# Eight of eleven chunks as seven products in three feed-forward layers, with a ring home for the half-width units and the norm's buffer as an eleventh slot

## The chip, the cores and the metric

The kernel runs on one core of a Trainium2 chip. The metric is the device time of one execution in microseconds (us); three runs of the kernel before gave 1053.86, 1053.05 and 1052.99, with a median of 1053.05. The engines are PE (matrix products; PEld is the loading of its stationary operand), DVE and ACT (elementwise work), POOL (a little elementwise work) and SP (issues the DMAs).

## The reference

Two layers over a residual stream x of 256 rows by 1024. Layer 0 mixes with forgetting attention (FoX), layer 1 with latent attention (MLA), whose shared key and value side is computed once from the x that leaves layer 0.

```python
def swiglu(x, w_in, w_out):                 # D_FF = 2816
    h = x @ w_in
    gate, up = h[..., :D_FF], h[..., D_FF:]
    return (silu(gate) * up) @ w_out

for i in range(2):
    if i == 1: k_nope, k_rope, v = shared_kv(x, ...)      # kv_down and kv_up
    x = LN(ALPHA * x + 0.5 * swiglu(x, ffn1_w_in[i], ffn1_w_out[i]))
    x = LN(ALPHA * x + (fox if i == 0 else mla)(x, ...))
    x = LN(ALPHA * x + 0.5 * swiglu(x, ffn2_w_in[i], ffn2_w_out[i]))
    gate = sigmoid(x @ ple_w_gate[i] + ple_b_gate[i])
    x = LN(ALPHA * x + gate * (p[i] @ ple_w_proj[i]))     # "PLE"
```

## The kernel before

**Every product is three.** An operand in fp32 is split into a high part, written by ACT in the type fp32r (line 242), and a low part, which DVE gets by subtracting the high one (line 243). `mm3` then issues high by high, high by low and low by high (line 590 is each single matmul). x itself is transposed on PE and split in the same way into `xT` (lines 603 and 607).

**Weights are a stream.** They arrive in raw tiles of 1 MB (three buffers, issued on SP's queue) and are split in units of 1024 columns into ten slots, `hl0` to `hl9`. Some buffers that a stage does not need (`ota`, `otb`, `qk`, `fs`) are lent to the stream as further slots and reclaimed later. A raw buffer is free again when its last unit is split. The class `Stream` plans the order: it keeps a clock for each engine, and whenever PE has been given another three matmuls (`pump`, line 358) it emits the next split if the unit's raw tile should have arrived, a slot is free, and DVE and ACT are at most 1.6 us behind PE on its clocks. If PE needs a unit that is not split yet, the split is emitted at once (`use`, line 370). So the order of instructions on ACT and DVE is fixed when the program is built, by these clocks. The two attention stages have a written order (`FOX`, `ORDER`), in which splits stand as steps of their own.

**A feed-forward layer** (`ffn`, line 698) runs over 11 chunks of 256 hidden columns. Chunks 0 and 1 are made first by `H`: x is the stationary operand and the weights move, for the upper 128 rows (t = 0) and, after x's lower rows are transposed, for t = 1. Each of these chunks has four units, written here (chunk, unit): (0,0) to (0,3) and (1,0) to (1,3). Chunks 2 to 10 are made by `HT` in three groups, (2,3,4), (5,6,7), (8,9,10): 96 matmuls of 128x256 each.

**The way back to 1024 columns** exists in two forms. `W` (line 906) takes a chunk's activations as stationary operand and multiplies with two units of `w_out`: eight products of 128x512, so 24 matmuls. `sums` (line 835) does the same with seven products of sums, so 21 matmuls. For it DVE first adds the activations (`add`, lines 820 to 825, in a tile `P`), splits 896 columns of them into a "home" (one of `ota`, `otb`, `qk`, `fs`), and adds the weights in the raw tile and a tile `ts` (lines 274, 280, 282); a chunk's weights are then four units, three of 1024 columns and one of 512 (key `ws`). The sums run in two batches, behind the first and the second group of `HT`; `combine` then adds the seven results into x. The chunks that use `W` are the last three, 8 to 10, and those in `early`: 0, 1 and 2 in the first layer (`cold`), 0 and 1 in layer 1's first feed-forward (`kv`, where the key and value work runs too), and 1 in the two second feed-forwards. `W` runs at the end for t = 0, then the norm of x's upper rows (`ln`, `ln_apply`, line 682), then `W` for t = 1 and the norm of the lower rows. The norm's gain and bias lie in a tile `gb`, loaded at chunk 4 (`load_gb`).

**Behind layer 0's second feed-forward** stand the PLE (line 1025) with eight units `pg` 0 to 7, and the `kv` layer's start. `post` (line 1049) multiplies the sigmoid, which ACT makes, with the projected embedding and takes the norm's statistics; `ln_apply` follows. In this stretch the units of `kv_down` (`kd` 0 to 3, 640 columns) and the first units of `H` are split too, between the norms.

## Time and profile before

| what | value |
| --- | --- |
| median of three runs | 1053.05 us (1052.99 to 1053.86) |
| the profiled execution: time, span | 1056.31 us, 1054.5 us |
| granted PE clock in it | 0.999 |
| busy in the span: PE, DVE, ACT, POOL | 1043.3, 872.7, 584.5, 57.5 us |
| read from HBM | 200.55 MB, 191 GB/s over the span |

The span is the part of the execution that the profile covers; 1.8 us of the execution lie around it. A row of a group of instructions gives the line, the engine, the operation, output and inputs by the program's names, the shape, the count, then busy us and mean ns of one, then the idle time of the engine ahead of them and what ended it. A row of a timeline gives start and length in us and, in square brackets, the idle time just before. A matmul's length in these rows holds its fill and drain; neighbours overlap, so their pace is read from the starts.

### The profile page before, as it was taken

The page shows a single profiled execution, that of the slowest core. Times are in us where ns is not written, and L with a number is a line of the kernel's source. Part 1 is how long each engine was busy: PE and PEld are TensorE (multiplying, and loading weights), DVE is VectorE, ACT ScalarE, POOL GpSimd, SP SyncE. Part 2 cuts the span into 40 slices and gives each one's busy share as a digit, 9 for nine tenths or more (in the row PEclk, how much of TensorE's full clock was granted, in tenths as well). Part 3 has the DMA queues.
Part 4 walks back from the last instruction along what each step waited for, and adds up shares of the span by engine and source line. Part 5 has one row for each costly group of instructions (what it writes and reads, how often), then busy time and mean ns, then how long its engine had stood idle before and what let it go on. Part 6 is the DMA issues. An engine that isn't in the chain of part 4 may idle for free.

```text
span 1054.5 us, 17598 instructions
## 1 busy us (share of the span) xinstructions
PE 1043.3 (99%) x7097; PEld 955.8 (91%) x7097; DVE 872.7 (83%) x1280; ACT 584.5 (55%) x889; POOL 57.5 (5%) x88
## 2 busy tenths in 40 slices
PE   9999999999999999999999999999999999999996
PEld 8999898999889999998899999988999889899986
DVE  5797976868898989968978898778887989899776
ACT  5555554556745555663564655536776564656621
POOL 0000000122400000000130000000000000000000
PEclk9999999999999999999999999999999999999999
DMA  7765486444637373764574637633444565555622
GB/s 279 284 228 208 160 277 246 155 146 151 221 132 275 139 259 134 256 232 159 179 274 158 240 125 248 235 109 105 151 155 165 188 213 194 199 197 213 208 113 80
DMA packets 37477, 202.75 MB, mean 192 GB/s; under 512 B 3970, under 2 KB 9874, under 8 KB 16532
## 3 DMA queue, kind: packets, MB, share of 16 engines
q1 hardware_dynamic: 37396, 201.63, 53.9%
q8 instruction: 56, 0.92, 0.3%
q14 instruction: 25, 0.20, 0.1%
HBM read 200.55 MB, written 1.06 MB: 191 GB/s over the span
## 4 chain that ended last, share of the span: by engine, by line
PE 71%; DVE 2%; ACT 1%; issue 0%; DVEq 0%; ACTq 0%
PE h L590 37%; PE y L590 23%; PE tr L590 8%; PE tr L594 2%; PE h L594 0%; DVE hl L243 0%; DVE x L682 0%; DVE tr L1688 0%; ACT qk L603 0%; ACT P L1313 0%; DVE h L1295 0%; DVE y L1295 0%; DVE hl L254 0%; ACT xT L1606 0%; DVE PT L607 0%
## 5 line engine op out<-in xcount | busy, mean ns | idle before, releaser
L590 PE MATMUL h<-xT,hl 128*128 128x256 f32 x3384 | 397.0, 279 | 0.2 <-DVE hl L303 0.2
L590 PEld LDWEIGHTS h<-xT,hl 128*128 128x128 f32 x3384 | 393.4, 189 | 1.9 <-ACT xT L603 0.6
L243 DVE TENSOR_TENSOR hl<-raw,hl 128x1024 fp32r<-128x1024 f32 (+3 forms) x289 | 336.3, 1195 | 52.5 <-ACT hl L242 51.1
L242 ACT ACTIVATE hl<-raw 128x1024 fp32r<-128x1024 f32 (+3 forms) x289 | 286.3, 1030 | 75.6 <-PE y L590 31.8
L590 PE MATMUL y<-hl,g 128*128 128x512 f32 x432 | 100.3, 390 | 0.0
L590 PEld LDWEIGHTS y<-hl,g 128*128 128x128 f32 x432 | 80.6, 188 | 16.3
L590 PE MATMUL y<-hl,otb 128*128 128x512 f32 x264 | 70.2, 398 | 0.0
L590 PE MATMUL h<-hl,xT 128*128 128x512 f32 (+2 forms) x300 | 65.2, 370 | 0.0
L590 PEld LDWEIGHTS h<-hl,xT 128*128 128x128 f32 x300 | 52.5, 188 | 9.3
L590 PEld LDWEIGHTS y<-hl,otb 128*128 128x128 f32 x264 | 48.2, 188 | 10.3 <-DVE otb L607 0.3
L254 DVE TENSOR_TENSOR hl<-raw,hl 128x1024 fp32r<-128x1024 f32 (+2 forms) x42 | 50.2, 1199 | 1.5 <-ACT hl L250 1.4
L590 PE MATMUL y<-hl,ota 128*128 128x512 f32 x192 | 49.9, 394 | 0.0
L674 POOL TENSOR_TENSOR rs<-ve,mhalf 128x1 f32<-128x1 f32 x16 | 15.1, 944 | 621.3 <-DVE ve L673 621.3
L590 PE MATMUL y<-hl,xT 128*128 128x512 f32 (+3 forms) x258 | 47.8, 333 | 0.0
L250 ACT ACTIVATE hl<-raw 128x1024 fp32r<-128x1024 f32 (+2 forms) x42 | 43.1, 1029 | 6.8 <-DVE raw L282 5.6
L603 ACT ACTIVATE xT<-tr 128x512 fp32r<-128x512 f32 x28 | 16.2, 597 | 53.2 <-PE tr L594 53.1
L590 PE MATMUL tr<-xT,hl 128*128 128x256 f32 x384 | 45.6, 278 | 0.0
L590 PEld LDWEIGHTS tr<-xT,hl 128*128 128x128 f32 x384 | 44.9, 188 | 0.3
L243 DVE TENSOR_TENSOR hl<-ts,hl 128x1024 fp32r<-128x1024 f32 (+1 forms) x47 | 43.4, 958 | 2.0 <-ACT hl L242 2.0
L799 ACT ACTIVATE P<-h 128x512 f32<-128x512 f32 x33 | 19.7, 598 | 45.1 <-PE h L590 45.0
L590 PEld LDWEIGHTS y<-hl,xT 128*128 128x128 f32 x258 | 39.8, 188 | 4.5 <-ACT xT L603 0.4
L590 PEld LDWEIGHTS y<-hl,ota 128*128 128x128 f32 x192 | 35.0, 188 | 6.6
(284 smaller groups left out, 1442.3 us busy)
## 6 DMA issues: line engine op xcount, KB each, us to landing
raw<-in_ffn_in_dram SPq DMA_DIRECT2D x85, 1024.0 KB, 4.9
raw<-in_ffn_out_dram SPq DMA_DIRECT2D x44, 1024.0 KB, 4.9
raw<-in_pg_dram SPq DMA_DIRECT2D x8, 1024.0 KB, 5.9
raw<-in_mo_dram SPq DMA_DIRECT2D x8, 1024.0 KB, 4.8
raw<-in_kq_dram SPq DMA_DIRECT2D x8, 640.0 KB, 3.9
gb<-in_ln_g_dram SPq DMA_DIRECT2D x8, 512.0 KB, 5.7
gb<-in_ln_b_dram SPq DMA_DIRECT2D x8, 512.0 KB, 6.5
raw<-in_fk_dram SPq DMA_DIRECT2D x4, 1024.0 KB, 5.4
```

The costliest lines, as they stand in the source:

```text
L242: nc.scalar.activation(hi, src, AF.Copy)
L243: nc.vector.tensor_tensor(lo, src, hi.bitcast(F32), op=ALU.subtract)
L250: nc.scalar.activation(hi, src, AF.Copy)
L254: nc.vector.tensor_tensor(lo, src, hi.bitcast(F32), op=ALU.subtract)
L590: self.nc.tensor.matmul(out, lhsT, rhs, start=start, stop=stop)
L594: self.nc.tensor.transpose(out, in_, self.ident)
L603: self.nc.scalar.activation(hi, src, AF.Copy)
L674: nc.gpsimd.tensor_tensor(rs, ve, self.mhalf, op=ALU.pow)
L799: nc.scalar.activation(gt, ps, AF.Silu)
```

## The change

- In the three feed-forward layers that are not `cold`, `early` is empty: chunks 0 to 7 all go by seven products. That converts chunk 1 in both second feed-forwards and chunks 0 and 1 in the `kv` layer, four chunks in all. The batches become (0,2,3,4) and (1,5,6,7).
- The homes are taken in the order `fs`, `qk`, `ota`, `otb`, in the `kv` layer too four of them; the last two are reclaimed only behind `H`.
- The unit of 512 columns (`ws` unit 3) no longer takes a slot but a tile of the `g4` ring (6 buffers of 4 KB).
- `gb` is lent to the stream from chunk 2 to chunk 8, as an eleventh slot, and the norm's gain and bias are loaded at chunk 10. This holds for the cold layer as well.
- In `add`, between ACT's high part and DVE's low part, a weight sum may be emitted (`between_sums`), where before only a waiting low part could.
- With other tags used first, the tiles move in memory: `ota` from byte 161248 to 178272 of a partition, `otb` from 178016 to 186720, `qk` from 186464 to 169696, `gb` from 169760 to 155104, `ts` from 155104 to 163552; `fs` stays.

```diff
@@ -43,7 +43,7 @@
 )
 ENDS = ((0, 512), (512, 768), (768, 1024))
 GROUPS = ((2, 3, 4), (5, 6, 7), (8, 9, 10))
-HOMES = ("ota", "otb", "qk", "fs")
+HOMES = ("fs", "qk", "ota", "otb")
 WS_ORDER = (1, 0, 2, 3)
 VRING = ((0, 0), (1, 1), (1, 2), (2, 2))
 FOX = (
@@ -138,7 +138,7 @@
     def pump(self, *a, **k):
         pass
 
-    lend = reclaim = check = load = busy = pair = follow = split = split_pieces = ahead = later = split_now = fill = pump
+    between_sums = lend = reclaim = check = load = busy = pair = follow = split = split_pieces = ahead = later = split_now = fill = pump
     between, hl, hold = {}, {}, False
 
 
@@ -179,6 +179,7 @@
         self.at = 0
         self.stop = None
         self.fixed = 80
+        self.side = False
 
     def load(self, n=NRAW):
         while self.loaded < len(self.groups) and self.loaded < self.done + n:
@@ -192,14 +193,14 @@
 
     def ahead(self):
 
-        if self.ready == len(self.order) or not self.slots or self.rest is not None:
+        if self.ready == len(self.order) or not self.free() or self.rest is not None:
             return
         if self.arrives.get(group_of(self.order[self.ready]), 1e12) <= self.pe_t + 500:
             self.split(half=True)
 
     def fill(self, n):
 
-        while self.ready < min(self.at + n, len(self.order)) and self.slots and group_of(self.order[self.ready]) in self.raw:
+        while self.ready < min(self.at + n, len(self.order)) and self.free() and group_of(self.order[self.ready]) in self.raw:
             self.split()
 
     def split_now(self):
@@ -224,9 +225,12 @@
         while self.sums_left(key):
             self.add(g)
         src, parts, n = unit_of(key, self.raw[g], self.sums.get(g))
-        slot = self.slots.pop(0)
-        self.slot_of[key] = slot
-        w = self.place(key, slot)
+        if self.aside(key):
+            w = self.pool.tile([128, 2, 512], F32R, tag="g4", name="g4", bufs=6)
+        else:
+            slot = self.slots.pop(0)
+            self.slot_of[key] = slot
+            w = self.place(key, slot)
         hi, lo = w[:parts, 0, :n], w[:parts, 1, :n]
         shape = src.shape
         if len(shape) == 3:
@@ -261,6 +265,22 @@
             both()
         self.pair(n)
         self.split_done(key, w)
+
+    def aside(self, key):
+        return self.side and key[0] == "ws" and key[-1] == 3
+
+    def free(self):
+        return self.slots or self.aside(self.order[self.ready])
+
+    def between_sums(self):
+
+        if self.rest is not None:
+            self.later()
+        elif self.ready < len(self.order) and not self.hold:
+            key = self.order[self.ready]
+            g = group_of(key)
+            if self.sums_left(key) and self.arrives.get(g, 1e12) <= self.pe_t + 500:
+                self.add(g)
 
     def sums_left(self, key):
         return key[0] == "ws" and self.added.get(group_of(key), 0) < 3
@@ -328,8 +348,8 @@
 
     def retire(self):
         if self.pending is not None and self.left[self.pending] == 0:
-            t = self.slot_of.pop(self.pending)
-            if t not in self.kept:
+            t = self.slot_of.pop(self.pending, None)
+            if t is not None and t not in self.kept:
                 self.slots.append(t)
         self.pending = None
 
@@ -357,7 +377,7 @@
 
     def pump(self):
 
-        if self.ready == len(self.order) or not self.slots or self.hold or self.order[self.ready] == self.stop:
+        if self.ready == len(self.order) or not self.free() or self.hold or self.order[self.ready] == self.stop:
             return
         arrival = self.arrives.get(group_of(self.order[self.ready]), 1e12)
         if arrival <= self.pe_t + 500 and max(self.act_t, self.dve_t) <= self.pe_t + SLACK_NS:
@@ -373,7 +393,7 @@
         i = self.index[key]
         self.at = max(self.at, i + 1)
         while self.ready <= i:
-            assert self.slots, (key, self.slot_of)
+            assert self.free(), (key, self.slot_of)
             self.split()
             self.pe_t = max(self.pe_t, self.dve_t)
         self.pump()
@@ -701,10 +721,11 @@
         nc, S = self.nc, self.S
         at = at or {}
         g, gT, forms = {}, {}, {}
-        homes = HOMES[:3] if kv else HOMES
-        S.reclaim(*homes)
-        S.fixed = 150
-        early = (0, 1, 2) if cold else (0, 1) if kv else (1,)
+        homes = HOMES
+        S.reclaim(*(homes if cold else homes[:2]))
+        S.fixed, S.side = 150, not cold
+        early = (0, 1, 2) if cold else ()
+        plain = early + tuple(range(NCH - STAG, NCH))
         summed = [c for c in range(NCH - STAG) if c not in early]
 
         def H(c, t, at=None, what=None, sweeps=0):
@@ -826,7 +847,7 @@
             S.busy(dve=700)
             tag, o = self.home(homes)
             self.high(o[:, 0, :], f[:, 128:1024])
-            S.later()
+            S.between_sums()
             self.low(o[:, 0, :], o[:, 1, :], f[:, 128:1024])
             forms[c] = tag, o
 
@@ -914,7 +935,7 @@
                             z[t][n],
                             lambda i: gT[c][:, i, 256 * kt + 128 * t : 256 * kt + 128 * t + 128],
                             lambda i: w[:, i, 512 * n : 512 * n + 512],
-                            (t, c, kt) == (0, early[0], 0), (c, kt) == (NCH - 1, 1),
+                            (t, c, kt) == (0, plain[0], 0), (c, kt) == (NCH - 1, 1),
                         )
 
         both = (0, 1)
@@ -935,6 +956,7 @@
                 self.kv_down(1)
             H(0, 1, sweeps=SW_H01)
             H(1, 1)
+            S.reclaim(*homes[2:])
         n = NCH
 
         turns = (
@@ -947,7 +969,12 @@
             for c in group:
                 for f in at.get(c, ()):
                     f()
-                if c == 4:
+                if c == 2:
+                    S.lend("gb")
+                if c == 8:
+                    S.reclaim("gb")
+                if c == 10:
+                    S.check("gb")
                     self.load_gb(li, lni)
                 if c == 10 and kv:
                     self.kv_transpose_rope()
@@ -960,7 +987,7 @@
             if i < 2:
                 if i == 1 and kv:
                     self.flush()
-                sums([c for c in summed if (c < 5) == (i == 0)], ("h", x))
+                sums([c for c in summed if (c < 5 and (cold or c != 1)) == (i == 0)], ("h", x))
                 x = 1 - x
             if i == 1:
                 S.lend(*after)
```

In the changed file the lines move: a matmul is line 610, a split's low part 247, the norm's four steps 702, the PLE's product with the sigmoid 1076.

Three places show how the order moves. The first is PE in layer 0's second feed-forward: chunk 1 on its way back to 1024 columns. Before, at the start of the last stage, it is 24 matmuls with the chunk's activations in `g4` and two units of `w_out`:

```order
L590 MATMUL y3_5059<-hl9_4891,g4_4131 128x512 x3
L590 MATMUL y0_5060<-hl9_4891,g4_4131 128x512 x3
L590 MATMUL y1_3984<-hl9_4891,g4_4131 128x512 x3
L590 MATMUL y2_3985<-hl9_4891,g4_4131 128x512 x3
L590 MATMUL y3_5059<-hl0_4903,g4_4131 128x512 x3
L590 MATMUL y0_5060<-hl0_4903,g4_4131 128x512 x3
L590 MATMUL y1_3984<-hl0_4903,g4_4131 128x512 x3
L590 MATMUL y2_3985<-hl0_4903,g4_4131 128x512 x3
```

After, in the second batch of sums, with the activations' sums in `fs`, three units in slots and the fourth in the ring:

```order
L610 MATMUL y1_3992<-hl3_4336,fs_4141 128x512 x3
L610 MATMUL y2_3993<-hl3_4336,fs_4141 128x512 x3
L610 MATMUL h1_4528<-hl8_4348,fs_4141 128x512 x3
L610 MATMUL y3_3990<-hl8_4348,fs_4141 128x512 x3
L610 MATMUL tr0_3994<-hl5_4363,fs_4141 128x512 x3
L610 MATMUL y0_3991<-hl5_4363,fs_4141 128x512 x3
L610 MATMUL tr1_3995<-g4_4375,fs_4141 128x512 x3
```

Eight lines of three matmuls have become seven.

The second place is DVE in the last stage of the same layer, at the end of the norm of x's upper rows (x0) and the transposed copy of them. Before, `pg` 0 to 5 have been split ahead of this norm, and `pg` 6 and 7 (`hl1` and `hl4` here) stand behind it:

```order
L682 SCALAR_TENSOR_TENSOR x0_69<-x0_69,mv_5150,gb_3854 128x512
L682 SCALAR_TENSOR_TENSOR x0_69<-x0_69,rs_5152,gb_3854 128x512
L243 TENSOR_TENSOR hl1_5184<-raw_5082,hl1_5184 128x1024
L243 TENSOR_TENSOR hl4_5193<-raw_5082,hl4_5193 128x1024
L607 TENSOR_TENSOR xT_75<-tr0_5198,xT_75 128x512
L607 TENSOR_TENSOR xT_75<-tr1_5208,xT_75 128x512
L663 SCALAR_TENSOR_TENSOR x1_70<-x1_70,y1_3984 128x512
```

After, only `pg` 0 to 4 are split ahead of the norm; `pg` 5 (`hl8` here) stands between the two copies, and `pg` 6 and 7 behind the norm of x's lower rows (x1), where before `kd` 0 to 3 were:

```order
L702 SCALAR_TENSOR_TENSOR x0_69<-x0_69,mv_5157,gb_4925 128x512
L702 SCALAR_TENSOR_TENSOR x0_69<-x0_69,rs_5159,gb_4925 128x512
L627 TENSOR_TENSOR xT_75<-tr0_5197,xT_75 128x512
L247 TENSOR_TENSOR hl8_5207<-raw_5081,hl8_5207 128x1024
L627 TENSOR_TENSOR xT_75<-tr1_5212,xT_75 128x512
L683 SCALAR_TENSOR_TENSOR x1_70<-x1_70,y1_3992 128x512
L684 BN_STATS st_5222<-x1_70 128x6
```

The third place is DVE in layer 0's PLE and at the `kv` layer's `H`. Before, behind the norm of x0, it splits (0,0) to (0,2) (`hl7`, `otb`, `qk`), copies xT, splits (0,3) (`fs`) and (1,0) (`hl2`), and then starts on the PLE's product for x1, which the norm of x1 follows:

```order
L243 TENSOR_TENSOR hl7_5371<-raw_5196,hl7_5371 128x1024
L243 TENSOR_TENSOR otb_5380<-raw_5196,otb_5380 128x1024
L243 TENSOR_TENSOR qk_5391<-raw_5281,qk_5391 128x1024
L607 TENSOR_TENSOR xT_75<-tr0_5394,xT_75 128x512
L607 TENSOR_TENSOR xT_75<-tr1_5401,xT_75 128x512
L243 TENSOR_TENSOR fs_5414<-raw_5281,fs_5414 128x1024
L243 TENSOR_TENSOR hl2_5425<-raw_5295,hl2_5425 128x1024
L1049 TENSOR_TENSOR g4_5429<-g4_5429,ota_5012 128x512
L663 SCALAR_TENSOR_TENSOR x1_70<-x1_70,g4_5429 128x512
```

After, `kd` 3 (`hl1`) comes behind the norm of x0, then (0,0) to (0,2) (`hl9`, `hl4`, `hl3`) around the copy, and then at once the product for x1:

```order
L247 TENSOR_TENSOR hl1_5387<-raw_5210,hl1_5387 128x640
L247 TENSOR_TENSOR hl9_5395<-raw_5291,hl9_5395 128x1024
L627 TENSOR_TENSOR xT_75<-tr0_5398,xT_75 128x512
L627 TENSOR_TENSOR xT_75<-tr1_5405,xT_75 128x512
L247 TENSOR_TENSOR hl4_5418<-raw_5291,hl4_5418 128x1024
L247 TENSOR_TENSOR hl3_5429<-raw_5322,hl3_5429 128x1024
L1076 TENSOR_TENSOR g4_5433<-g4_5433,ota_5056 128x512
```

and (0,3) (`otb`) and (1,0) (`hl8`) come behind that product's norm:

```order
L702 SCALAR_TENSOR_TENSOR x1_70<-x1_70,rs_5444,gb_5237 128x512
L702 SCALAR_TENSOR_TENSOR x1_70<-x1_70,mv_5442,gb_5237 128x512
L702 SCALAR_TENSOR_TENSOR x1_70<-x1_70,rs_5444,gb_5237 128x512
L1443 TENSOR_SCALAR ve_5480<-ss_5479 128x1
L247 TENSOR_TENSOR otb_5510<-raw_5322,otb_5510 128x1024
L247 TENSOR_TENSOR hl8_5515<-raw_5390,hl8_5515 128x1024
```

On PE nothing moves here: its order is the kd products, then (0,0), (0,1), (0,2), (0,3), (1,0) in both kernels.

## The prediction

> **What bounds the kernel now.** I read the page's busy shares first, then the waits of PE, then the groups of one shape, and last the timelines of PE and DVE at the places where the order moves. The page's first part (busy us, share, instructions):
>
> ```profile
> PE 1043.3 (99%) x7097; PEld 955.8 (91%) x7097; DVE 872.7 (83%) x1280; ACT 584.5 (55%) x889; POOL 57.5 (5%) x88
> ```
>
> The waits of PE (what waits for what: us in all, times, longest us):
>
> ```profile
> PE y L566 <- POOL mhalf L551: 1.2, 1, 1.2
> PE h L590 <- DVE PT L607: 0.7, 2, 0.5
> PE h L590 <- ACT p L603: 0.5, 1, 0.5
> PE h L590 <- DVE otb L607: 0.2, 1, 0.2
> PE h L590 <- DVE hl L303: 0.2, 1, 0.2
> ```
>
> PE is busy for 1043.3 of 1054.5 us, and its named waits add up to 1.2 + 0.7 + 0.5 + 0.2 + 0.2 = 2.8 us. So nearly each matmul taken away shortens the run by its pace, and nearly each new wait of PE lengthens it; almost no old stall is there to go. DVE has 17% of the span free, but not everywhere. A fifth of a percent, 2.1 us, is about what a measurement of this kernel tells from no change.
>
> **What is removed from PE.** Four chunks go from 8 to 7 products of three matmuls: 12 matmuls of 128x512 fewer. The group of that shape in the last stage (us busy, mean ns of one):
>
> ```profile
> L590 PE MATMUL y<-hl,g 128*128 128x512 f32 x432 | 100.3, 390 | 0.0
> ```
>
> 100.3 / 432 = 0.232 us each, since neighbours overlap: 12 x 0.232 = 2.8 us. Gain: -2.8.
>
> The Trainium skill ("TensorE: Matmul & The Clock Gate", Back-to-back issue gap) gives about 131 ns as the sustained spacing of 512-column matmuls. By it the 12 would be worth 1.6 us, and the sum below would come to 1056.7 in place of 1055.5. The trace does not agree: 232 ns here, so the row decides.
>
> **The homes.** The batch of sums in layer 0's second feed-forward, on PE's timeline (start, length), one home after the other, 21 matmuls each:
>
> ```profile
> 413.16 1.54 PE L590 MATMUL y<-hl,ota 128*128 128x512 f32 x6
> ...
> 417.94 1.56 PE L590 MATMUL y<-hl,otb 128*128 128x512 f32 x6
> ...
> 422.82 1.56 PE L590 MATMUL y<-hl,qk 128*128 128x512 f32 x6
> 424.22 0.87 PE L590 MATMUL h<-hl,qk 128*128 128x512 f32 x3
> ...
> 427.70 0.87 PE L590 MATMUL h<-xT,hl 128*128 128x256 f32 x6
> ```
>
> From start to start `ota` takes 4.78 us and `otb` and `qk` 4.88 each, 228 against 232 ns a matmul, with the same work: what differs is the buffer. The change gives `ota`, `otb` and `qk` other addresses, and which of them will be slow no row shows. 24 chunks are summed in the three layers: all from the faster to the slower pace would be 24 x 0.10 = +2.4 us, all the other way -2.4. Both paces are mixed before, and nothing says that they won't be mixed after, so half of that, -1.2 to +1.2, for the range; I take +0.1.
>
> The Trainium skill ("SBUF — State Buffer", SBUF: two separate sides) says that on the engines' side only the port pair of the vector and GpSimd engines causes contention. By it a home's address costs nothing and this term is 0 without a range; the 0.10 us between two homes is left unexplained by it.
>
> **What is added to DVE.** The groups by shape:
>
> ```profile
> L243 DVE TENSOR_TENSOR hl<-raw,hl 128x1024 fp32r<-128x1024 f32 x266 | 317.0, 1222 | 51.1 <-ACT hl L242 49.9
> ...
> L274 DVE TENSOR_TENSOR ts<-raw 128x1024 f32<-128x1024 f32 x25 | 30.6, 1223 | 0.5
> ...
> L280 DVE TENSOR_TENSOR ts<-ts,raw 128x512 f32<-128x512 f32 x25 | 17.3, 692 | 0.9
> ...
> L243 DVE TENSOR_TENSOR hl<-ts,hl 128x512 fp32r<-128x512 f32 x23 | 15.8, 686 | 1.0 <-ACT hl L242 1.0
> ...
> L820 DVE TENSOR_TENSOR P<-P 128x256 f32<-128x256 f32 x25 | 10.6, 425 | 2.7 <-ACT P L773 1.9
> L607 DVE TENSOR_TENSOR g<-P,g 128x512 fp32r<-128x512 f32 x15 | 10.4, 691 | 7.7 <-ACT g L603 7.7
> ...
> L607 DVE TENSOR_TENSOR qk<-P,qk 128x896 fp32r<-128x896 f32 x7 | 7.6, 1089 | 3.1 <-ACT qk L603 3.1
> ...
> L825 DVE TENSOR_TENSOR P<-P 128x128 f32<-128x128 f32 x25 | 7.3, 292 | 0.9
> ```
>
> Per converted chunk: weight sums 1.22 + 2 x 0.69, splits of the sums 3 x 1.22 + 0.69, activation sums 0.43 + 2 x 0.29 and their low part 1.09; less two splits of `w_out` (2 x 1.22) and the low part of 512 columns (0.69): +5.9 us, 23.7 in all. Of this 8.4 us fall before the batch's end (the two splits of `w_out` came later), and the batch gets 21 x 0.232 = 4.9 us longer on PE. So DVE's lead there shrinks by 3.5 us in each second feed-forward and by 7.0 in the `kv` layer, if its idle time stays. The lead before, at the last chunk's unit for the fourth product: DVE splits it, PE reads its low part one matmul after the start shown above (424.22):
>
> ```profile
> 420.91 1.22 DVE L243 TENSOR_TENSOR hl<-raw,hl 128x1024 fp32r<-128x1024 f32 x1
> ```
>
> that is 424.45 - 422.13 = 2.3 us; and in the `kv` layer, DVE then PE:
>
> ```profile
> 630.31 1.22 DVE L243 TENSOR_TENSOR hl<-raw,hl 128x1024 fp32r<-128x1024 f32 x1
> ```
>
> ```profile
> 635.49 0.87 PE L590 MATMUL h<-hl,qk 128*128 128x512 f32 x3
> ```
>
> 635.72 - 631.53 = 4.2 us. Without reclaimed idle time the leads would be -1.2, -1.2 and -2.8: 5.2 us of stalls, the upper end. But the group of `HT` ahead of the batch, where PE runs on its own, leaves DVE idle (window, PE, PEld, DVE busy, ..., granted clock, DMA share, GB/s):
>
> ```profile
> 380.00:413.20 33.20, 33.20 (x294) 33.16 (x294) 27.45 (x32) 19.15 (x23) 0.00 (x0) 1.00 0.58 215
> ...
> 427.70:460.80 33.10, 33.10 (x293) 33.10 (x292) 28.09 (x31) 18.84 (x22) 0.95 (x1) 1.00 0.70 251
> ```
>
> ```profile
> 543.70:576.80 33.10, 33.10 (x294) 33.10 (x293) 27.50 (x34) 15.56 (x19) 0.00 (x0) 1.00 0.54 191
> ...
> 591.30:624.40 33.10, 33.10 (x293) 33.09 (x292) 27.25 (x33) 17.56 (x21) 0.00 (x0) 1.00 0.55 190
> ```
>
> 33.2 - 27.45 = 5.8 us before the batch in the second feed-forward, and 5.6 and 5.9 us before the two of the `kv` layer. That is more than 3.5, and 11.5 is more than 7.0; the eleventh slot, the ring and the sums in ACT's gaps let the stream run ahead into it. Lower end 0. I take +0.7, near the lower end, since the idle time is larger than the need in each of the three places but part of it waits for ACT or PE.
>
> ACT gets a 1024-column high part more per chunk and stays near 56%; the DMAs move the same bytes. The norm's gain and bias now load in the third group, where the DMA share is already 0.70 (last row of the first pair): 0 in the sum (rival 3).
>
> **What moves: the `kv` layer's `H`.** More splits in the batches leave the stream behind at the end of layer 0's second feed-forward: `pg` 5 to 7, `kd` 0 to 3 and the units of `H` are split later, and (0,3) and (1,0) come to stand behind the PLE's product and norm of x1 on DVE. DVE before, at the places between which the order moves:
>
> ```profile
> 489.08 0.69 DVE L607 TENSOR_TENSOR xT<-tr,xT 128x512 fp32r<-128x512 f32 x1 [0.34 <-ACT xT L603]
> ...
> 495.39 0.75 DVE L682 SCALAR_TENSOR_TENSOR x<-x,rs,gb 128x512 f32<-128x512 f32 x1
> 496.06 3.03 DVE L243 TENSOR_TENSOR hl<-raw,hl 128x640 fp32r<-128x640 f32 x4
> 499.00 1.28 DVE L607 TENSOR_TENSOR xT<-tr,xT 128x512 fp32r<-128x512 f32 x2
> 501.46 0.69 DVE L1049 TENSOR_TENSOR g<-g,ota 128x512 f32<-128x512 f32 x1 [1.18 <-ACT g L1048]
> ...
> 513.91 1.21 DVE L243 TENSOR_TENSOR fs<-raw,fs 128x1024 fp32r<-128x1024 f32 x1
> ...
> 516.18 0.68 DVE L1049 TENSOR_TENSOR g<-g,ota 128x512 f32<-128x512 f32 x1
> ...
> 523.34 0.75 DVE L682 SCALAR_TENSOR_TENSOR x<-x,rs,gb 128x512 f32<-128x512 f32 x1
> 524.01 0.15 DVE L1416 TENSOR_SCALAR ve<-ss 128x1 f32<-128x1 f32 x1
> ```
>
> and PE's first use of (0,3), `fs` in that run:
>
> ```profile
> 521.35 1.54 PE L590 MATMUL h<-fs,xT 128*128 128x512 f32 x6
> ```
>
> Before, (0,3) was done at 513.91 + 1.21 = 515.1, and PE read its low part at 521.35 + 0.23 = 521.6, 6.5 us later. After, DVE has this to do. Between the copies of xT a split of 1.22 comes in where 0.34 was idle, so the norm of x1 that ended at 496.1 ends at 497.0. Then `pg` 6 and 7 (2.4), two xT copies (1.3), `kd` 0 to 2 (3/4 of 3.03 = 2.3), product and norm of x0 (as for x1 below, 7.9), `kd` 3 (0.8), (0,0) (1.1, as half of 513.91 to 516.18, where two splits follow each other), xT (1.3), (0,1) and (0,2) (2.3), product and norm of x1 (516.18 to 524.09: 7.9), a small one (0.1) and (0,3) (1.2): 28.6 us, all on one in-order engine, to 525.6. PE stands at (0,3) from 521.6: 4.0 us. Behind it in PE's queue is all the rest, so the run is longer by that. Lower end 3.0 (the 0.9 taken up by idle time ahead), upper end 5.2 (the product of x0 waits for ACT's sigmoid by 1.18 as before, at 501.46, since the high parts of `kd` 0 to 2 stand ahead of it on ACT). Part of it may show as PE's transposes of x0 waiting for the later norm. I take +4.1. Nothing hides it: PE has no other work in its order. (1,0) is read by its high part first, which ACT has made long before.
>
> In layer 1's PLE the same lag puts two units (2.4 us) behind the norm of x0 and ahead of the xT copies, which PE awaits; idle time there covers most. Between 0 and 1.2, I take +0.3. FoX and MLA keep their written orders, the cold layer its sums: 0, with a change of pace by place of tiles inside the range of the homes.
>
> **Sum**: -2.8 + 0.1 + 0.7 + 4.1 + 0.3 = +2.4 us. The profiled execution would be 1056.3 + 2.4 = 1058.7; it ran 3.3 above the median, so the median goes from 1053.05 to **1055.5**.
>
> **Rivals.**
> 1. *The late unit is covered* (faster). If DVE reaches (0,3) by 521.6, 4.0 us sooner than summed, the 4.1 vanish: 1051.4, and 1050.4 if the batches and the last PLE cost nothing either. For it: DVE's free 17% and the 6.5 us of lead before. Against: all of the 28.6 us stand in a row between two points, a norm that waits for PE's results and PE's own arrival; no idle time is in the sum to take out. From 4 us less it decides. Chance 0.10.
> 2. *The batches run dry* (slower). Leads of -1.2, -1.2 and -2.8 as above: 5.2 in place of 0.7: 1060.0. For it: leads of 2 to 4 us are short against 3.5 to 7.0 of new work. Against: 5.6 to 5.9 us of idle time in each group ahead. Chance 0.18.
> 3. *The norm's gain and bias come late* at chunk 10, in the stage with a DMA share of 0.70. Us to landing, from the page's DMA issues:
>
> ```profile
> raw<-in_ffn_in_dram SPq DMA_DIRECT2D x85, 1024.0 KB, 4.9
> ...
> gb<-in_ln_b_dram SPq DMA_DIRECT2D x8, 512.0 KB, 6.5
> ```
>
> Behind three raw tiles on SP's queue they would be there 3 x 4.9 + 6.5 = 21.2 us after the load is reached. PE then has chunk 10 (a third of 33.1: 11.0) and 36 matmuls of `W` (8.4): 19.4. So 1.8 us late, in four layers 7.2: 1062.7. Against: the norm's statistics come first and don't read them. Chance 0.03.
> 4. *The saving doesn't come or comes double*, as the pace of 128x256 matmuls in the groups shifts with the tiles' places: the 2% between the homes, on one group of 33.1 us, is 0.7 us, and on three 2.0: 1053.5 to 1057.5. For it: the homes' rows. Against: `xT`, which moves in these matmuls, keeps its place. Chance 0.09.
>
> **How the numbers follow.** The forecast (late unit 3 to 5 us, batches nearly dry but held) has 0.60 and its own range 1053.6 to 1057.5. The range over all takes in rival 1's upper half at the low end and most of rival 2 at the high: 1051.2 to 1059. Faster than 1050.95: 0.08, most of rival 1. Slower than 1055.16: rivals 2 and 3, half of 4, and half of the forecast: 0.18 + 0.03 + 0.05 + 0.31 = 0.57. Within: the rest, 0.35.
>
> **What would show it.** In PE's waits of the changed kernel one of 3 to 5 us for a low part (line 247) at `H` of the `kv` layer, near 520 us, with the norm's rows (702) just ahead of the split on DVE. No wait above 1 us in the batches of sums, near 425, 635 and 958. PE's busy time less by 2.8, or by the 12 matmuls' count. It is wrong if that wait is under 2 us, or if other waits add up to more than it.

## The result and the profile after

| kernel | median us (runs) | ratio to before, 95% interval |
| --- | --- | --- |
| before | 1053.02 (8) | |
| after | 1055.62 (8) | 1.0032 [1.0018, 1.0045] |
| after, once more beside the experiments | 1055.22 (8) | 1.0023 [1.0013, 1.0033] |

The change makes the kernel slower by 2.4 to 2.6 us; 1055.5 was forecast. Here and below two executions are left out that took far longer than all others (one of before with 2692 us, one of the version "ahead and shifted" with 1479). The profiled execution of after took 1054.48 us, with a span of 1052.7, and so is shorter than the one shown of before (1056.31). Both are single executions, and they differ most in the first layer, whose order of instructions the change leaves alone (more on that below). So the two are compared by stretches, from one place of the program to another. Behind layer 0's attention nearly all of these repeat to 0.02 us between two profiles of before, and between two of after, wherever the granted clock is full; the largest exception is 0.19 us, in one stretch of after.

The page of after, first part:

```profile
PE 1037.3 (99%) x7085; PEld 949.7 (90%) x7085; DVE 895.0 (85%) x1312; ACT 592.5 (56%) x901; POOL 59.9 (6%) x88
```

The waits of PE in after:

```profile
PE h L610 <- DVE otb L247: 3.0, 1, 3.0
PE y L586 <- POOL mhalf L571: 1.2, 1, 1.2
PE tr L614 <- DVE x L702: 0.7, 1, 0.7
PE h L610 <- DVE PT L627: 0.6, 2, 0.4
PE h L610 <- ACT p L623: 0.5, 1, 0.5
PE h L610 <- DVE otb L627: 0.2, 1, 0.2
PE h L610 <- DVE hl L323: 0.2, 1, 0.2
```

The first and the third row are new; the others were there before, or have their like. DVE in after at layer 0's PLE and the `kv` layer's `H`:

```profile
484.55 1.22 DVE L247 TENSOR_TENSOR hl<-raw,hl 128x1024 fp32r<-128x1024 f32 x1 [0.26 <-ACT hl L246]
...
491.99 0.75 DVE L702 SCALAR_TENSOR_TENSOR x<-x,rs,gb 128x512 f32<-128x512 f32 x1
492.66 2.35 DVE L247 TENSOR_TENSOR hl<-raw,hl 128x1024 fp32r<-128x1024 f32 x2
...
498.85 0.69 DVE L1076 TENSOR_TENSOR g<-g,ota 128x512 f32<-128x512 f32 x1 [0.43 <-ACT g L1075]
...
506.70 1.96 DVE L247 TENSOR_TENSOR hl<-raw,hl 128x640 fp32r<-128x640 f32 x2
...
509.77 2.35 DVE L247 TENSOR_TENSOR hl<-raw,hl 128x1024 fp32r<-128x1024 f32 x2
512.04 0.68 DVE L1076 TENSOR_TENSOR g<-g,ota 128x512 f32<-128x512 f32 x1
...
519.20 0.75 DVE L702 SCALAR_TENSOR_TENSOR x<-x,rs,gb 128x512 f32<-128x512 f32 x1
519.87 0.15 DVE L1443 TENSOR_SCALAR ve<-ss 128x1 f32<-128x1 f32 x1
519.93 1.22 DVE L247 TENSOR_TENSOR otb<-raw,otb 128x1024 fp32r<-128x1024 f32 x1
```

PE there, from the PLE's products with `pg` 6 to the first matmul of chunk 2:

```profile
494.10 3.00 PE L610 MATMUL y<-hl,xT 128*128 128x512 f32 x12
...
506.93 0.63 PE L614 MATMUL tr<-ident,x 128*128 128x128 f32 x4 [0.71 <-DVE x L702]
...
517.82 0.40 PE L610 MATMUL h<-otb,xT 128*128 128x512 f32 x1
521.20 1.43 PE L610 MATMUL h<-otb,xT 128*128 128x512 f32 x5 [2.99 <-DVE otb L247]
...
543.42 0.86 PE L610 MATMUL tr<-xT,hl 128*128 128x256 f32 x6
```

The rows run as the order had it: `pg` 5 between the xT copies (484.55), `pg` 6 and 7 behind the norm of x1 (492.66), the product and norm of x0 (498.85 to 506.70), `kd` 3 with (0,0), then (0,1) and (0,2), then the product for x1 (512.04) and its norm. The split of (0,3), `otb`, begins at 519.93, straight behind that norm, whose last step is the row at 519.20. PE has read the high part at 517.82 and stands until 521.20: 2.99 us. The 0.71 at 506.93 is the transposes of x0 waiting for its norm. From 494.10 to 543.42 this stretch takes 49.32 us; before it is, between the same two matmuls,

```profile
498.48 3.00 PE L590 MATMUL y<-hl,xT 128*128 128x512 f32 x12
...
543.66 0.86 PE L590 MATMUL tr<-xT,hl 128*128 128x256 f32 x6
```

45.18 us. The difference is 4.14 us. In the three layers where chunks were converted PE is faster: 0.3 us in layer 0's second feed-forward, 1.4 in the `kv` layer, 0.7 in layer 1's second one, 2.3 in all. For each converted chunk `W` is shorter by 5.44 us and a batch longer by 4.75 to 4.79; in layer 0's second feed-forward the second group of `HT` also takes 33.54 us where it took 33.12. The batches hold: no wait of PE is in any of them. In layer 0's second one, PE from home to home and the split that is read last in time:

```profile
409.51 1.52 PE L610 MATMUL y<-hl,fs 128*128 128x512 f32 x6
...
414.27 1.52 PE L610 MATMUL y<-hl,qk 128*128 128x512 f32 x6
...
419.03 1.56 PE L610 MATMUL y<-hl,ota 128*128 128x512 f32 x6
...
423.91 1.56 PE L610 MATMUL y<-gb,otb 128*128 128x512 f32 x6
...
428.79 0.87 PE L610 MATMUL h<-xT,hl 128*128 128x256 f32 x6
```

```profile
422.28 1.22 DVE L247 TENSOR_TENSOR gb<-raw,gb 128x1024 fp32r<-128x1024 f32 x1
```

`fs` and `qk` take 4.76 us each, `ota` and `otb` 4.88. The unit `gb` is split by 423.50 and its low part read at 423.91 + 0.23: a lead of 0.6 us, where the one shown of before was 2.3.

### The profile page after: what moved, and what is told of

Same layout as the page of the kernel before. It is cut to its first block, busy times and chain, and to the rows that moved or that the text cites. A ratio compares the mean times of both kernels' runs of the same rounds, so it can differ in the third digit from the quotient of the medians.

```text
span 1052.7 us, 17554 instructions
## 1 busy us (share of the span) xinstructions
PE 1037.3 (99%) x7085; PEld 949.7 (90%) x7085; DVE 895.0 (85%) x1312; ACT 592.5 (56%) x901; POOL 59.9 (6%) x88
## 4 chain that ended last, share of the span: by engine, by line
PE 68%; DVE 3%; ACT 1%; issue 1%; POOL 0%; DVEq 0%; ACTq 0%; POOLq 0%
PE h L610 37%; PE y L610 21%; PE tr L610 8%; PE tr L614 2%; DVE hl L247 1%; DVE x L702 0%; PE h L614 0%; DVE x L683 0%; DVE st L684 0%; DVE g L1076 0%; ACT hl L246 0%; POOL rs L694 0%; DVE tr L1715 0%; ACT qk L623 0%; ACT P L1340 0%
## 5 line engine op out<-in xcount | busy, mean ns | idle before, releaser
L610 PE MATMUL h<-xT,hl 128*128 128x256 f32 x3144 | 366.9, 278 | 0.2 <-DVE hl L323 0.2
L610 PEld LDWEIGHTS h<-xT,hl 128*128 128x128 f32 x3144 | 362.8, 189 | 2.0 <-ACT xT L623 0.6
L247 DVE TENSOR_TENSOR hl<-raw,hl 128x1024 fp32r<-128x1024 f32 (+4 forms) x273 | 317.3, 1191 | 38.8 <-ACT hl L246 37.6
L246 ACT ACTIVATE hl<-raw 128x1024 fp32r<-128x1024 f32 (+4 forms) x273 | 270.0, 1027 | 72.0 <-DVE raw L302 41.0
L610 PE MATMUL y<-hl,g 128*128 128x512 f32 x336 | 78.6, 391 | 0.0
L610 PEld LDWEIGHTS y<-hl,g 128*128 128x128 f32 x336 | 62.6, 188 | 12.6
L610 PE MATMUL y<-hl,otb 128*128 128x512 f32 x219 | 58.0, 399 | 0.0
L610 PE MATMUL y<-hl,xT 128*128 128x512 f32 (+3 forms) x282 | 52.7, 334 | 0.0
L610 PEld LDWEIGHTS y<-hl,otb 128*128 128x128 f32 x219 | 39.8, 188 | 8.3 <-DVE otb L627 0.3
L294 DVE TENSOR_TENSOR ts<-raw 128x1024 f32<-128x1024 f32 x29 | 35.4, 1222 | 0.6
```

Of the source, the lines that this page charges most:

```text
L246: nc.scalar.activation(hi, src, AF.Copy)
L247: nc.vector.tensor_tensor(lo, src, hi.bitcast(F32), op=ALU.subtract)
L294: tt(s[:, 0:1024].rearrange("p (a b) -> p a b", b=512), r[:, 0:512][:, None, :].to_broadcast([128, 2, 512]), r[:, 512:1536].rearrange("p ( ...
L610: self.nc.tensor.matmul(out, lhsT, rhs, start=start, stop=stop)
```

## The experiments

Times in us. "H" is the stretch of PE just shown, from the product with `pg` 6 to chunk 2's first matmul. "Clock" is the lowest granted clock in a window of 4 us at 516 to 532. H, the waits and the clock are of one profiled execution each. The last three rows have a single run each, so their times by themselves tell little.

| kernel | median (runs) | ratio to before | H | PE's waits in H | clock |
| --- | --- | --- | --- | --- | --- |
| before, once more | 1052.39 (10) | 0.9998 [0.9989, 1.0007] | 45.2 | none | 1.00 |
| after, once more | 1055.22 (8) | 1.0023 [1.0013, 1.0033] | 49.3 | 0.7, 3.0 | 1.00 |
| (0,3) ahead | 1051.91 (11) | 0.9996 [0.9987, 1.0005] | 47.3 | 0.7, 0.5, 0.2 | 1.00 |
| kd behind the norm, (0,3) ahead | 1055.15 (11) | 1.0025 [1.0016, 1.0034] | 50.9 | 1.4, 0.6, 0.9 | 0.57 |
| layer 0's chunk 1 by `W` | 1051.29 (11) | 0.9986 [0.9977, 0.9995] | 45.1 | none | 1.00 |
| all by `W` | 1052.69 (11) | 0.9992 [0.9982, 1.0001] | 45.1 | none | 1.00 |
| homes shifted | 1053.56 (11) | 1.0007 [0.9998, 1.0016] | 50.8 | 0.8, 3.0 | 0.70 |
| ahead and shifted | 1049.81 (4) | 0.9966 [0.9952, 0.9979] | 47.6 | 0.8, 0.9 | 1.00 |
| layer 0 by `W`, shifted | 1049.37 (11) | 0.9968 [0.9959, 0.9977] | 45.0 | none | 1.00 |
| no eleventh slot | 1057.06 (1) | | 50.9 | 0.7, 3.0 | 0.57 |
| no ring | 1055.72 (1) | | 50.9 | 0.7, 3.0 | 0.63 |
| no sums in gaps | 1056.59 (1) | | 50.9 | 0.7, 3.0 | 0.75 |

### Both kernels once more

No edit.

> The kernel before, unchanged, once more: what one execution differs from another by. In the profiles of before and after the first 122 us differ by 3.5 us, in a layer whose order is the same in both. If that is a property of the execution, this profile may show either: chunk 5 of the first layer begins at 71.0 us (as in the profile of after) or 73.5 us (as in that of before), or between. If it were a property of the changed layout, it must show 73.5 again. Time against itself: ratio 1.000, and the width of its interval shows what the others can tell.

The profile had chunk 5 of the first layer at 70.2 us, near after's 71.0, and the ratio to itself was 0.9998. So the first layer's 3.5 us belong to the execution and don't need the changed layout; from layer 0's second feed-forward to layer 1's PLE the stretches were those of the first profile of before.

> After, unchanged, once more, on the chip of the three runs below. The stage starts behind the first layer, which repeat to 0.02 us between executions, differ between before and after by +1.8 us in all: about 1054.4 here if that is the whole effect (before at 1052.7). If the 0.32% of the first comparison holds, 1056.0, and something that the stage starts of one profile don't show adds 1.5 us. The two waits of 3.0 and 0.7 us must be there again.

1055.22 lies halfway between the two. The waits of 3.0 and 0.7 were there again, and H took 49.3 once more.

### One split moved ahead

```diff
             for k in range(8):
                 if k == 6:
                     self.XT(0)
                 gate(1, k, full)
+            S.fill(8)
             for c0, c1 in full:
                 post(1, c0, c1)
```

On DVE one instruction moves, (0,3) to ahead of the product for x1; two neighbours further on change places.

> After, with one split moved: unit (0,3) of the kv layer is split ahead of the PLE's product for x1. Theory (the late unit): PE's wait of 3.0 us for that unit goes, the 0.7 us for x0's norm stays, the time falls by 3.0 us from 1055.6 to 1052.6, about the kernel before. Rival (the slowdown is a pace or clock of the whole run): the wait goes from the list but the time stays at 1055.6. Rival (the stall moves on): x1's norm is 1.1 us later, and PE's transposes of x1 wait up to 1 us for it; 1053.6.

PE around there:

```profile
505.89 0.63 PE L614 MATMUL tr<-ident,x 128*128 128x128 f32 x4 [0.71 <-DVE x L702]
...
516.77 1.55 PE L610 MATMUL h<-otb,xT 128*128 128x512 f32 x6
...
519.75 2.14 PE L610 MATMUL h<-hl,xT 128*128 128x512 f32 x8 [0.51 <-ACT hl L246]
...
525.24 0.73 PE L610 MATMUL h<-ota,xT 128*128 128x512 f32 x2 [0.16 <-DVE ota L247]
```

The wait for (0,3) is gone (516.77 has none), and the time falls to that of before. But H is only 2.0 us shorter, not 3.0: PE now waits 0.5 us for the high part of (1,1), which ACT makes behind a silu that itself waits for PE, and 0.2 for the low part of (1,3), with smaller stops between. The rival that the stall moves on was right in part, at another unit than it named.

### The kd units behind the norm as well

```diff
         bias(0, full)
+        S.stop = None if last else ("kd", 0)
...
         self.ln_apply(0, st[0][0][:, 0:2, :], LN_EPS)
+        S.stop = None
```

in addition to the edit above.

> After, with (0,3) split ahead of the PLE's product for x1 as in the run before, and kd 0 to 3 all split behind x0's norm in place of kd 0 to 2 ahead of it. Theory: both waits go (3.0 and 0.7), x0's norm ends 1 us or more earlier, x1's norm ends at 522.2 against PE's second half of the transposes at 521.9, so up to 0.4 us may be left: 3.3 to 3.7 us less than after, 1051.9 to 1052.3. Rival: the 0.7 us does not depend on the three splits (ACT's sigmoid is last), then 1052.6 as in the run before.

This missed. Both old waits are gone, but H takes 50.9 us (about 1.6 of them by the clock), with

```profile
518.86 3.10 PE L610 MATMUL h<-hl,xT 128*128 128x512 f32 x12 [1.42 <-ACT hl L246]
...
525.41 0.74 PE L610 MATMUL h<-hl,xT 128*128 128x512 f32 x2 [0.59 <-DVE hl L247]
527.08 0.74 PE L610 MATMUL h<-ota,xT 128*128 128x512 f32 x2 [0.93 <-DVE ota L247]
```

The norm of x0 ends sooner, and what it gains is lost behind it: the units of chunk 1, next in the stream, are now the late ones. The clock falls too, but only in some executions: the granted clock over the whole span is 0.995 in the profiled one, the lowest of the eleven, and the four with 0.998 still have a median of 1055.1, so the miss is not the clock's. DVE and ACT have a fixed amount of work between x's norms and `H`; moving pieces of it changes which unit is late. The order was not the whole fault: the amount was.

### Which part of the change makes the stream late

```diff
-        early = (0, 1, 2) if cold else ()
+        early = (0, 1, 2) if cold else (1,) if li == 0 else ()
```

> After, but chunk 1 of layer 0's second feed-forward goes by W as before (eight products); the three other converted chunks stay. Theory (the 8.4 us of DVE work that this one conversion puts ahead of the last stage make the stream late): (0,3) is split ahead of the PLE's product again, both waits are gone, and of the 12 matmuls' saving only that of 3 is given back: 3.7 + 0.4 - 0.3 = 3.8 us less than after. Rival (the eleventh slot, the ring or the order of the homes makes the stream late): the waits stay and the run is 0.3 us slower than after.

The longest waits of PE in this kernel, down to 0.4:

```profile
PE y L586 <- POOL mhalf L571: 1.2, 1, 1.2
PE h L610 <- ACT hl L321: 1.1, 1, 1.1
PE h L610 <- DVE PT L627: 0.6, 2, 0.4
PE h L610 <- ACT p L623: 0.5, 1, 0.5
PE h L610 <- DVE P L826: 0.4, 1, 0.4
```

No wait for line 247 is left, and H takes 45.1 us as before. The time is 1051.3, where 1055.6 - 3.8 = 1051.8 was expected. So one conversion out of four, the one just ahead of the stretch, costs all that is lost, and the other three are worth having (1.4 us against before, by the stretches of their two layers). The 0.4 us for `P` (line 826) comes up at 567.9, in the `kv` layer's first group of `HT`, ahead of its first batch.

```diff
-        early = (0, 1, 2) if cold else ()
+        early = (0, 1, 2) if cold else (0, 1) if kv else (1,)
```

> All of the change but the conversions: early is (1,) or (0,1) as before; homes in the new order and four in the kv layer, the ring for the half-width unit, the norm's buffer as a slot, weight sums in ACT's gaps stay. Theory: none of these costs or gains by itself, the matmuls are those of before: 1052.7 within 0.5. Rival (the norm's late load or the moved buffers cost): 1053.5 to 1055, with new waits at the norms or longer steps from stage to stage.

1052.69, ratio 0.9992: what is left of the change, the slot, the ring and the homes' order, neither costs nor gains in the time that the runs could show. By stretches it does a little: the second group of layer 0's second feed-forward takes 33.40 us in place of 33.12, and the end 0.4 more (below).

### The homes' address

```diff
+        if tag == "qk" and "qk" not in self.seen:
+            self.seen.add("qk")
+            self.tl([128, 32], F32, "gap4", 1)      # 128 bytes ahead of ota
...
+        if not self.rec and "st" not in self.seen:
+            self.seen.add("st")
+            self.tl([128, 32], F32, "gap5", 1)      # 128 bytes behind otb
```

> After, with a gap of 128 bytes ahead of ota and one of 128 bytes behind otb: these two buffers lie 128 bytes higher, every buffer behind them 256 bytes, the order of the instructions is the same. Theory (the address sets the pace): ota and otb go from 4.88 us for a chunk's 21 matmuls to 4.76 as fs and qk; 12 chunks of the three layers, so 1.4 us less, some more where these two hold weights: 1053 to 1054.2. Rival (the pace belongs to what is written in them or to the order): 4.88 stays, 1055.6.

```profile
419.52 1.52 PE L615 MATMUL y<-hl,ota 128*128 128x512 f32 x6
...
424.28 1.52 PE L615 MATMUL y<-gb,otb 128*128 128x512 f32 x6
...
429.04 0.87 PE L615 MATMUL h<-xT,hl 128*128 128x256 f32 x6
```

`ota` and `otb` now take 4.76 us each, 419.52 to 424.28 to 429.04, as `fs` and `qk` do. All homes that take 4.76 to 4.78 us, in any kernel here, start at a byte that leaves 224 when divided by 256, and all that take 4.87 or 4.88 (`otb` and `qk` before, `ota` and `otb` after) at one that leaves 96. The run without the eleventh slot (below) is a second test, since its buffers lie elsewhere: there `qk`, at 169568 (96), takes 4.87 us, and `ota` and `otb`, at 178144 and 186592 (224), 4.76. Against after, five of the six batches are shorter by 0.22 to 0.24 us and one by 0.07, MLA by 0.4 and the last PLE by 0.4. The median is 2.1 us lower than after's first and 1.7 lower than its second, and that although the clock falls in its profile. The wait of 3.0 us is still there.

### The versions that beat both

```diff
-            H(0, 0, None if kv else 12, S.ahead, SW_H00)
+            H(0, 0, 12, S.ahead, SW_H00)
```

with (0,3) ahead and the homes shifted. On ACT, the high part of (1,1) goes ahead of the silu.

> After with three edits: (0,3) split ahead of the PLE's product for x1, the high part of (1,1) made on ACT ahead of the silu's table load, and ota and otb 128 bytes higher. The run that moved only (0,3) lost 3.0 us of wait but got waits of 0.5 (ACT, high part of (1,1)) and 0.2 in return. Theory: the 0.5 goes too, and the homes give 1.4 as in the run with the shift alone: 1051.9 - 0.5 - 1.4 = 1050.0, faster than both kernels. Rival: another unit of H is late next, 1050.5 or more; or the shift gains nothing in the time, as the first layer's pace varies, 1051.4.

```profile
524.47 0.74 PE L615 MATMUL h<-ota,xT 128*128 128x512 f32 x2 [0.94 <-DVE ota L247]
```

1049.81, ratio 0.9966. The shift gave what it gave alone; the third edit did not: the wait for (1,1) went, and (1,3) is late by 0.9 in its place. H is 47.6, not below the 47.3 without that edit. This was the rival's first half.

The last one joins the two edits that worked: layer 0's chunk 1 by `W`, and the shift.

> The run with layer 0's chunk 1 by W, with ota and otb 128 bytes higher as well. Theory: the two effects add: 1051.3 - 1.4 = 1049.9 (0.9972 of before), and by the stage starts behind the first layer 4.8 us less than after, where the run with the split ahead and the shift has 3.9. Rival: with other addresses the one wait of 0.4 us in the kv layer's first batch grows, 1050.5 or more.

1049.37, ratio 0.9968; H 45.0; behind layer 0's attention 5.2 us less than after. The effects add. It is as fast as the version before it and simpler.

### What fed the batches

```diff
-                if c == 2:
-                    S.lend("gb")
-                if c == 8:
-                    S.reclaim("gb")
-                if c == 10:
-                    S.check("gb")
+                if c == 4:
                     self.load_gb(li, lni)
```

> After without gb as a slot: the norm's gain and bias load at chunk 4 as before. In after the smallest lead of DVE over PE in the second batch of layer 0's second feed-forward is 0.6 us, so the batch holds with nothing to spare. Theory (the slot feeds the batches): without it the stream runs ahead less, and a wait of 0.3 to 1.2 us comes up in a second batch. Rival (slots are not what limits the stream, DVE's work is): no wait in a batch, steps as in after.

```diff
-        S.fixed, S.side = 150, not cold
+        S.fixed, S.side = 150, False
```

> After with the half-width unit in a slot again in place of the ring. Theory (slots feed the batches): two slots fewer in a batch, waits of 0.3 to 1.2 us in the second batches. Rival (DVE's work is the limit): no wait in a batch, steps as in after.

```diff
-            S.between_sums()
+            S.later()
             self.low(o[:, 0, :], o[:, 1, :], f[:, 128:1024])
```

> After without weight sums between ACT's high part and DVE's low part of the activation sums. Each such place leaves DVE waiting for ACT by about 1.0 us (1.02 at 394.43 in the profile of before), two or three of them ahead of a second batch's end. Theory (DVE's idle time is what the batches live on): the lead of 0.6 us is used up, a wait of 0.4 to 2 us in the second batch of layer 0's second feed-forward. Rival: another split takes the gap anyway, no wait.

No wait came up in any batch of the three. The last edit changes nothing: the program it builds is that of after, instruction for instruction, since `between_sums` never finds a sum to emit there. So the sums in gaps have no part in after's result, and this run is one more execution of after. The other two expectations missed. Without the slot the steps are those of after, but for the homes' pace and the end (both below); without the ring the `kv` layer takes 0.4 us more and MLA 1.0 more, with a wait of 0.7 at 713.9. So neither the slot nor the ring alone keeps the batches from running dry. What the three share with after is the wait of 3.0 us in `H`, and here they showed something more. The kernel without the ring, 1 us windows from that wait on (PE, PEld, DVE, ACT, POOL busy, granted clock, DMA share, GB/s):

```profile
517.00:518.00 1.00, 0.00 (x0) 0.00 (x0) 0.96 (x2) 0.41 (x1) 0.00 (x0) 1.00 0.00 0
...
520.00:521.00 1.00, 1.00 (x6) 0.82 (x5) 1.00 (x2) 0.00 (x0) 0.94 (x1) 1.00 0.69 98
521.00:522.00 1.00, 1.00 (x4) 0.75 (x3) 1.00 (x2) 0.92 (x2) 1.00 (x1) 0.51 0.68 221
522.00:523.00 1.00, 1.00 (x4) 0.77 (x3) 0.71 (x2) 1.00 (x2) 0.92 (x3) 0.50 0.98 418
523.00:524.00 1.00, 1.00 (x4) 0.81 (x3) 1.00 (x2) 0.35 (x1) 1.00 (x1) 0.50 1.05 434
524.00:525.00 1.00, 1.00 (x5) 0.78 (x5) 1.00 (x1) 0.00 (x0) 1.00 (x2) 0.79 1.08 401
525.00:526.00 1.00, 1.00 (x10) 0.91 (x9) 0.25 (x1) 0.14 (x1) 0.90 (x3) 1.00 0.93 377
```

PE is idle from 516.6 to 519.6 and works again from there; 1.4 us later the granted clock is 0.50, for 3.4 us (half of that is lost: 0.49 + 0.50 + 0.50 + 0.21), and full again before 525. H takes 50.9 in place of 49.3: 1.6 us more, behind the wait and not in it. Of the six profiles with the 3.0 us wait, four show it (0.57 to 0.75 in a 4 us window). Three of the six are of one program (after, its repeat, and no sums in gaps), and only the last of these shows it.

## Why the prediction was right, and where its terms were off

- **What bounds the kernel**: right. PE is 99% busy, and the time followed PE's matmuls, waits and clock.
- **The late unit** (+4.1): right in place, cause and size. The stretch is 4.14 us longer, by waits of 2.99 for (0,3) and 0.71 for the norm of x0, which the prediction had said might show apart, and 0.4 where PE starts again behind them. The 2.99 lies at the very lower end of the 3.0 to 5.2 given; it is the two waits together that make the 4.1. The split ended at 519.93 + 1.22 = 521.15 in after, 28.5 us after the norm of x1 (492.66); the sum had 28.6. Undoing the one conversion takes all of it away.
- **The conversion** (-2.8): -2.7 by its own rows. The 24 matmuls of `W` take 5.44 us, 0.227 each and not 0.232, and the batches grew by 4.75 to 4.79 for each chunk. The layers together gained only 2.3 us in the profile of after and 2.5 in its repeat, since the second group in layer 0's second feed-forward lost 0.4 and 0.2 (33.54 and 33.34 us for 33.12). About 0.2 of it stands in both profiles, 27.8 us into the group, where PE's weight loads wait 0.14 us for `P` of DVE (line 826); the rest stays open.
- **The homes** (+0.1, -1.2 to +1.2): the pace does follow the address. It came to 0: of the four homes after, two have the 4.88 and two the 4.76, and the batches of three before had the 4.88 twice as well. The term was worth more as a remedy (1.2 us in the batches, and 0.4 each in MLA and the last PLE) than as a cost.
- **The batches** (+0.7): 0 in the batches, and the 0.2 just named ahead of one. Rival 2 did not happen. The lead fell from 2.3 to 0.6 and not to -1.2. DVE's idle time in that layer, from chunk 2 to the batch's end, went from 11.6 to 10.4 us, which is 1.2 of the 1.8 between; the rest isn't traced. That the slot, the ring and the sums in gaps would let DVE do so was my reason for a low value. The sums in gaps never took place, and the runs without the slot or the ring do not bear the reason out singly; both left out together wasn't tried.
- **The last PLE** (+0.3): no wait came up. After ends 0.4 us later behind DVE's last instruction, and so does the kernel with all by `W`. Of all changed versions only the run without the eleventh slot does not: 8.4 us from PE's last matmul to the end, as in before, where the others have 8.8. So the 0.4 comes with that slot, or with the place in memory that `gb` has by it; how stays open.
- **Rival 1** (covered): no. **Rival 3** (the norm's load): no wait at any norm for `gb`. **Rival 4** (pace in the groups): the nine groups of the three layers take the same to 0.02 us, but for the one named above.
- **The signs**: the wait, its place and the 12 matmuls fewer came as named. Two signs were badly chosen. PE's busy time fell by 6.0 us in the two profiles shown and by 0.7 between their repeats, so a single pair doesn't measure 2.8. And the other waits of after add up to 3.4 us, more than the 3.0, though 2.8 stood in before already; only new waits should have counted.
- **What the sum left out**: the clock behind the wait. The stretches add up to 4.1 - 2.3 + 0.4 = +2.2 us, less 0.3 to 0.6 in FoX, where some buffers moved: +1.6 to +1.9. The medians say +2.4 to +2.6. An estimate of the clock's part: of the sixteen timed executions of after, six had a granted clock of 0.994 or 0.995 over the span, and every version without a wait of 1 us in `H` had at least 0.997; six of sixteen at 1.6 us are 0.6 us on average, or more, since one fall can leave the figure at 0.997, as in the run without the ring. So part of the agreement to 0.1 us is luck: the batches' 0.7, which didn't come, stood in for a clock that I had not thought of.

## What to carry to other kernels

When one engine is full, price a change by what it adds to the others just ahead of a place where they are busy without a break, here two norms in a row; in this kernel the matmuls saved were seen in each of the three layers, the splits they cost almost only there. If a unit is late by the amount of work, moving single splits makes the next one late; take the work away at that place and keep the change elsewhere. And count a wait of 3 us on PE as possibly more than its length: here 1.6 us more, in some executions.

## What the runs showed of the hardware

- **The clock behind a wait.** After 3.0 us of idle PE the granted clock was 0.50 for 3.4 us in four of six profiles, beginning 0.2 to 1.4 us after PE had resumed, and cost 1.6 us. The traces suggest what decides. In each profile with a fall behind the waits in `H`, the fall begins a whole number of steps of 3.413 us ahead of the clock's last fall at the kernel's end (without the ring 521.01 and 1050.08, which is 155 steps; 154 in the three others). Counted back in such steps from the kernel's end, the wait lies for 2.0 to 3.0 us inside one step in those four, and the clock falls at that step's end; in after and its repeat a step ends amid the wait (1.5 and 1.5 us; 1.2 and 1.9), and it does not fall. The run with waits of 1.4, 0.6 and 0.9 us within 10 us fits less well: it fell behind a step (152 from the end) that held only the last two, 1.5 us. So that the place of the wait in the steps matters is likely, but the amount that a step needs is not shown. The Trainium skill ("TensorE: Matmul & The Clock Gate", What's actually happening) has such a clock: half speed after an idle window of about 3.4 us that runs freely. The half, the 3.4 us and the free run fit the rows; but here PE was not idle for the whole of such a window in any of the five.
- **A stationary operand's address sets the pace.** 226.7 ns a matmul of 512 columns at bytes that leave 224 of 256, 232.4 at those that leave 96; 128 bytes of padding moved two buffers from one to the other and saved 0.12 us per chunk, and the run without the eleventh slot agrees with its own addresses. What lies behind it no run shows.
- **Two paces in the first layer.** In PE's windows of 75 to 100 us, of the first profile of before and of its repeat, with the same program and a granted clock of 1.00 in both:

```profile
75.00:100.00 25.00, 25.00 (x215) 25.00 (x214) 17.91 (x23) 10.46 (x12) 0.00 (x0) 1.00 0.65 242
```

```profile
75.00:100.00 25.00, 25.00 (x223) 25.00 (x223) 18.88 (x23) 13.44 (x16) 0.00 (x0) 1.00 0.64 228
```

215 matmuls against 223. It changes from execution to execution, in both kernels, and ends by 124 us; between these two profiles the way from the first group of `HT` to the third takes 93.6 and 91.3 us, 2.3 apart. Its cause stays open.
